# RWKV-7 rank-32 products as one split single-pass matmul with the terms stacked in the partitions

## The chip, the cores and the metric

The kernel runs on one core of a Trainium2 chip. The metric is the device time of one execution in microseconds (us). Before the change it is 1765.97 us, the median of two runs (1765.7 and 1766.24). The engines are named as the profile names them: PE (TensorE matmul), PEld (its weight load), DVE (VectorE), ACT (ScalarE), POOL (GpSimd) and SP (SyncE, which only issues DMAs). PSUM is the memory into which PE writes.

## The reference

One layer with two token mixers side by side and a gated MLP behind them, for 128 context tokens and 1024 latent tokens (1152 columns, d_model 1024). The part that changes is in the RWKV-7 mixer: decay and in-context learning rate come out of three products of rank 32.

```python
u_b = dwconv1d(u_b, p['rwkv_conv'])
r, k, v, wdf, wdb, ad, gd = jnp.split(u_b, idx, axis=-1)
w_f = jnp.exp(-DECAY_SCALE * jax.nn.sigmoid(p['rwkv_w0'][0] + jnp.tanh(wdf) @ p['rwkv_w2'][0]))
w_b = jnp.exp(-DECAY_SCALE * jax.nn.sigmoid(p['rwkv_w0'][1] + jnp.tanh(wdb) @ p['rwkv_w2'][1]))
a = jax.nn.sigmoid(p['rwkv_a0'] + ad @ p['rwkv_a2'])
```

`wdf`, `wdb` and `ad` have 32 channels each, `rwkv_w2` is 2 x 32 x 512 and `rwkv_a2` is 32 x 512. All is float32.

## The kernel before

**Stages.** Channels lie in the partitions and tokens in the columns. After the norm and the modulation, the input is kept twice, as `hh` (rounded to float32r, a float32 form that PE takes in one pass) and `hl` (the rest). A projection (`proj`, lines 1061 to 1073) loads 128 columns of a weight, splits them into `wh` and `wl` in the same way, and adds three single-pass products per 128 rows of the contraction and 384 tokens: `hh,wh`, `hl,wh` and `hh,wl` (lines 1070, 1071, 1072). So the large products already run in split form. The order of stages is: modulation and first columns; projections and features of four head pairs; HGRN2 and RWKV-7 scans; output projection; MLP.

**Features.** `features(p, r, k, v)` runs once for each of four pairs p and three blocks tb of 384 tokens, twelve blocks in all. In each block there are two places with rank-32 products. The first, which is called **a** here, is line 1331's input: `small_proj(wlora[64:96, cb], twt[64:96, c])`, one matmul with 32 contraction rows (it is recorded at line 1299). The second, called **dec** here, is a group of two such matmuls at line 1364, one for each direction, on partitions 0 to 31 and 32 to 63. Both operands are plain float32. `twt` (128 x 1152, memory `low`) holds the 96 features, and `wlora` (memory `fx`) the 96 rows of weights. Behind a and dec stand tanh on ACT, a scan and products on DVE, 24 small matmuls per direction (lines 1397 and 1398), and stores of the finished features. `elim` then inverts triangular systems: 31 pairs of steps on DVE (lines 1441 and 1444) and small matmuls (lines 1462 and 1464).

**What sets the order.** The program is first recorded as operations with their dependencies. Three tables then decide it: `SEQUENCE` is the order in which all operations are issued, `ENGINE_OF` names the engine where an operation has a choice (a copy on ACT, DVE or POOL; a store on POOL or SP), and `PLACE_OF` names the buffer. Each engine takes its instructions strictly in that order; semaphores hold them back. Memory is laid out by hand in large tiles (`low`, `top`, `fx`, `qm` and others); a name such as `ta` or `nb` is a place or two in one of them.

## Time and profile before

| what | value |
|---|---|
| median of the runs | 1765.97 us |
| profiled execution, its own time | 1769.48 us |
| span of the profiled execution | 1767.7 us |
| PE busy | 1708.6 us, 97% |
| PEld busy | 1539.8 us, 87% |
| DVE busy | 1434.8 us, 81% |
| ACT busy | 936.8 us, 53% |
| POOL busy | 350.5 us, 20% |
| mean granted PE clock | 0.998 |

The span runs from the first to the last instruction. A float32 matmul has two records in the profile, a float32r matmul one. Busy time of a group is the time in which at least one of its instructions ran. A row `L1299 PE MATMUL banks<-low,fx 32*128 32x384` is the operation of line 1299 on PE, writing PSUM (`banks`) from `low` and `fx`, with a weight of 32 rows and 128 columns and 384 moving columns. `low<-x` with an engine's q (SPq, POOLq) is a DMA issued there.

### The profile page before, as it was taken

Reading aid. Unit: us, or ns where it says so; the run is one execution under the profiler, and the core shown is the slowest. Engines: PE = TensorE matmul, PEld = TensorE weight load, DVE = VectorE, ACT = ScalarE, POOL = GpSimd, SP = SyncE. Lnnn points to the kernel's source line nnn. Section 1 sums busy time; section 2 is a strip of 40 time slices with the busy share of each in tenths; the row PEclk is TensorE's granted clock in tenths of the full one; section 3 lists DMA queues with packets and bytes.
Section 4 is the critical chain, followed back from the end, with each engine's and each line's share of the span. In section 5 each row is a group of like instructions: output and inputs, shape, how many; then the busy total and the mean of one; then the engine's idle time right before and its main releaser. Section 6 shows DMA issues by size and latency. Waiting matters only on the chain.

```text
span 1767.7 us, 44608 instructions
## 1 busy us (share of the span) xinstructions
PE 1708.6 (97%) x17726; PEld 1539.8 (87%) x17726; DVE 1434.8 (81%) x2742; ACT 936.8 (53%) x1955; POOL 350.5 (20%) x543
## 2 busy tenths in 40 slices
PE   6999999999999999999999999999999999999998
PEld 4888888888988888888778899999999999878787
DVE  5648889977779988886879797888988888878766
ACT  5657576663255656664556764444444444554542
POOL 0003141352222011112110122232333322000000
PEclk9999999999999999999999999999999999999999
DMA  8426365486777788989997757777877777896775
GB/s 278 137 72 164 89 162 139 112 232 195 203 207 221 212 246 278 288 271 289 296 288 264 215 122 153 155 157 160 165 156 153 146 162 149 282 306 218 229 231 183
DMA packets 342068, 352.97 MB, mean 200 GB/s; under 512 B 73180, under 2 KB 264565, under 8 KB 341508
## 3 DMA queue, kind: packets, MB, share of 16 engines
q1 hardware_dynamic: 287508, 282.27, 53.0%
q0 software_dynamic: 54352, 67.85, 19.6%
q8 instruction: 139, 2.28, 0.5%
q14 instruction: 69, 0.57, 0.1%
HBM read 254.99 MB, written 118.10 MB: 211 GB/s over the span
## 4 chain that ended last, share of the span: by engine, by line
PE 55%; DVE 18%; DMA 15%; issue 5%; ACT 4%; SPq 1%; POOL 1%; DVEq 0%; ACTq 0%; POOLq 0%
PE banks L2065 14%; PE banks L1070 6%; PE banks L1072 5%; PE banks L1071 5%; PE banks L2229 5%; DVE low L2153 3%; DMA low<-in_ffn_w_up_dram 2%; DMA wr<-in_ffn_w_down_dram 2%; PE banks L1955 1%; PE banks L1957 1%; PE banks L1956 1%; DMA d_t<-in_ffn_w_down_dram 1%; DMA low<-d_a 1%; DMA wr<-in_ffn_w_up_dram 1%; DMA wr<-d_o 1%
## 5 line engine op out<-in xcount | busy, mean ns | idle before, releaser
L1070 PE MATMUL banks<-hh,wh 128*128 128x384 f32 x768 | 278.5, 363 | 4.4 <-DVE fx L1250 3.1
L1072 PE MATMUL banks<-hh,wl 128*128 128x384 f32 x768 | 257.8, 336 | 0.0
L1071 PE MATMUL banks<-hl,wh 128*128 128x384 f32 x768 | 257.5, 335 | 0.0
L2153 DVE SCALAR_TENSOR_TENSOR low<-low,pf 128x1024 f32<-128x1024 f32 x176 | 225.4, 1281 | 7.9 <-ACT low L2147 5.2
L2065 PE MATMUL banks<-qm,wh 128*128 128x320 f32 x968 | 224.1, 310 | 0.2 <-ACT fx L2102 0.2
L2065 PE MATMUL banks<-hbm,wh 128*128 128x256 f32 x880 | 164.4, 283 | 3.6 <-DVE low L2123 1.9
L2065 PE MATMUL banks<-qm,wl 128*128 128x320 f32 x528 | 162.9, 308 | 0.2 <-DVE wl L2035 0.2
L1070 PEld LDWEIGHTS banks<-hh,wh 128*128 128x128 f32 x768 | 144.3, 188 | 20.5 <-issue 8.5
L2065 PEld LDWEIGHTS banks<-qm,wh 128*128 128x128 f32 x968 | 160.7, 189 | 0.5 <-ACT fx L2102 0.4
L1071 PEld LDWEIGHTS banks<-hl,wh 128*128 128x128 f32 x768 | 144.6, 188 | 2.7 <-issue 1.4
L1072 PEld LDWEIGHTS banks<-hh,wl 128*128 128x128 f32 x768 | 144.2, 188 | 0.0
L2065 PEld LDWEIGHTS banks<-hbm,wh 128*128 128x128 f32 x880 | 139.1, 190 | 5.2 <-DVE low L2123 2.5
L2065 PE MATMUL banks<-ham,wh 128*128 128x256 f32 (+1 forms) x616 | 132.0, 294 | 0.0
L2065 PE MATMUL banks<-hbm,wl 128*128 128x256 f32 x440 | 124.4, 283 | 0.6 <-DVE wl L2035 0.6
L2102 ACT COPY fx<-banks 128x256 f32<-128x256 f32 (+1 forms) x132 | 52.1, 398 | 108.1 <-PE banks L2065 101.3
L2065 PEld LDWEIGHTS banks<-ham,wh 128*128 128x128 f32 x616 | 101.5, 190 | 0.1
L2065 PEld LDWEIGHTS banks<-qm,wl 128*128 128x128 f32 x528 | 99.1, 188 | 0.6 <-DVE wl L2035 0.6
L2065 PEld LDWEIGHTS banks<-hbm,wl 128*128 128x128 f32 x440 | 83.9, 191 | 0.8 <-DVE wl L2035 0.8
L2173 POOL DMA_DIRECT2D d_t<-in_ffn_w_down_dram x44 | 45.0, 1050 | 183.9 <-DMA d_t<-d_t 139.9
L2035 ACT CAST wh<-wr 128x512 fp32r<-128x512 f32 x73 | 45.2, 622 | 66.2 <-PE banks L2065 28.6
L2035 ACT CAST wh<-low 128x512 fp32r<-128x512 f32 x81 | 50.0, 620 | 52.9 <-PE banks L2065 25.5
L2065 PE MATMUL banks<-ham,wl 128*128 128x256 f32 (+1 forms) x264 | 77.0, 292 | 0.0
(578 smaller groups left out, 4369.3 us busy)
## 6 DMA issues: line engine op xcount, KB each, us to landing
wr<-in_w_in_dram SPq DMA_DIRECT2D x34, 512.0 KB
d_t<-in_ffn_w_down_dram POOLq DMA_DIRECT2D x61, 256.0 KB, 5.8
low<-d_a SPq DMA_DIRECT2D x53, 256.0 KB
low<-d_ak SPq DMA_DIRECT2D x64, 192.0 KB
low<-d_kb SPq DMA_DIRECT2D x36, 256.0 KB
low<-in_ada_w_dram SPq DMA_DIRECT2D x32, 256.0 KB
fx<-in_ada_w_dram SPq DMA_DIRECT2D x16, 512.0 KB
top<-in_ada_w_dram SPq DMA_DIRECT2D x16, 512.0 KB
```

The source lines that it names most:

```text
L1070: mm(o, wh[:, kt, :], hh[:, kt, c], kt == 0, False)
L1071: mm(o, wh[:, kt, :], hl[:, kt, c], False, False)
L1072: mm(o, wl[:, kt, :], hh[:, kt, c], False, kt == KT - 1)
L1955: mm(ps, oh[:, kt, :], woh, kt == 0, False)
L1956: mm(ps, oh[:, kt, :], wol, False, False)
L1957: mm(ps, ol[:, kt, :], woh, False, kt == KT - 1)
L2035: split(*w, src)
L2065: pe.matmul(o, a[:, kt, :], b[:, kt, :], start=start and first, stop=last, skip_group_check=not start)
L2102: act.copy(keep[n], y[:, 0:w])
L2153: dve.scalar_tensor_tensor(av, shifted(dy, dx), tap(3 * dy + dx), av, MUL, ADD)
L2173: acc(td[j][k], b)
L2229: pe.matmul(o, x, y, start=fresh and f, stop=l, skip_group_check=not fresh)
```

## The change

The three terms of a split product (high by high, low by high, high by low) are put into the partitions, 32 rows each, so that one single-pass matmul with 96 contraction rows gives their sum.

- After tanh, the features of each token block are split: an ACT cast makes the high part and a DVE subtraction the low part. 27 stores (32 x 384 each, on POOL or SP) write them to a DRAM tensor `d_lo` in the order high, low, high for each of the three products.
- Each of the twelve blocks loads its 96 x 3 x 384 piece back into `lom` with a DMA on POOL. There is one such buffer, so the load of a block waits until dec of the block before has run.
- Each pair loads its 128 columns of `rwkv_w2` and `rwkv_a2` three times (six DMAs on SP), casts them on ACT into `w3` and subtracts on DVE in the third copy, which makes high, high, low. There is one buffer of `w3` in `lom` too.
- a and dec become one and two matmuls at line 1349 of the new kernel (function `lora`), all on partitions 0 to 95.
- `top` shrinks by 1536 columns to make room for `lom`; behind the features the same room is `topb`, and the first HGRN2 operation that may use it waits for all products (`lora_ops`). Some small buffers move; `wraw` has three places instead of four.
- All three tables are new.

```diff
@@ -120,337 +120,340 @@
 SEQUENCE = [int(i) for i in """
-0 12 13 14 11 2 15 16 27 1 17 18 19 4 20 22 28 29 33 3 24 30 39 23 31 32 34 35 36 40 37 38
...
@@ -795,7 +806,13 @@
-    top, qm = r1_.mem("top", N1), r1b.mem("qm", N1, F32R)
+    r1_.above.append(r2b)
+    top, qm = r1_.mem("top", NT1), r1b.mem("qm", N1, F32R)
+    lom, topb = r2a.mem("lom", NL, F32R), r2b.mem("topb", NL, box=r1_)
...
+    plan.tag("twt", [(lom, 0)], T)
+    plan.tag("wlora", [(lom, T)], 384)
...
@@ -1089,6 +1110,7 @@
+    lord = dram("d_lo", [96, 3, T])
...
@@ -1256,10 +1278,6 @@
-    wlora = tl("wlora", [P, 512])
-    for d in range(2):
-        ld(wlora[32 * d:32 * d + 32, :], I["rwkv_w2"][0, d])
-    ld(wlora[64:96, :], I["rwkv_a2"][0])
...
@@ -1293,6 +1311,14 @@
+    for tb in range(3):
+        c, lh, ll = slice(tb * 384, (tb + 1) * 384), tl("ta", [P, 384]), tl("nb", [P, 384])
+        act.copy(lh[0:96].bitcast(F32R), twt[0:96, c])
+        combine(ll[0:96].bitcast(F32R), twt[0:96, c], lh[0:96], SUB)
+        for j in range(3):
+            for a, t in enumerate((lh, ll, lh)):
+                st(lord[32 * a:32 * a + 32, j, c], t[32 * j:32 * j + 32, :])
+    lora_ops = []
...
@@ -1312,6 +1338,16 @@
+        raw3, w3 = tl("ta", [P, 3, P]), tl("wlora", [P, 3, P], F32R)
+        for a in range(3):
+            ld(raw3[32 * a:32 * a + 32, 0:2, :], I["rwkv_w2"][0].rearrange("d r c -> r d c")[:, :, cb])
+            ld(raw3[32 * a:32 * a + 32, 2, :], I["rwkv_a2"][0][:, cb])
+        act.copy(w3[0:96], raw3[0:96])
+        combine(w3[64:96], raw3[64:96], w3[64:96].bitcast(F32), SUB)
+
+        def lora(ps, j):
+            mm(ps, w3[0:96, j, :], lt[0:96, j, :], True, True)
...
@@ -1326,8 +1362,12 @@
+            lt = tl("twt", [P, 3, 384], F32R)
+            pool.dma_start(lt[0:96], lord[:, :, c].bitcast(F32R))
             ta, nb = tl("ta", [P, 384]), tl("nb", [P, 384])
-            ps = small_proj(wlora[64:96, cb], twt[64:96, c])
+            ps = pbank("sp")[:, 0:384]
+            lora(ps, 2)
...
@@ -1361,7 +1401,8 @@
-                    mm(dec[d], wlora[32 * d:32 * d + 32, cb], twt[32 * d:32 * d + 32, c], True, True)
+                    lora(dec[d], d)
```

**How the order moves.** On PE, in the first pair, dec of block 0 (two matmuls) and a of block 1 stand close together. `wh`, `wl`, `hh` and `hl` are the operands of a projection; between the rows shown only such projection matmuls stand, twelve in all before the change:

```order
L1072 MATMUL banks<-hh,wl_135 128x384
L1364 MATMUL banks<-low,fx 128x384 x2
L1070 MATMUL banks<-hh,wh_134 128x384
L1071 MATMUL banks<-hl,wh_134 128x384
L1072 MATMUL banks<-hh,wl_135 128x384
...
L1072 MATMUL banks<-hh,wl_135 128x384
L1299 MATMUL banks<-low,fx 128x384
```

After the change there are fifteen (lines 1091 to 1093 of the new kernel are 1070 to 1072 of the old):

```order
L1093 MATMUL banks<-hh,wl_137 128x384
L1349 MATMUL banks<-lom 128x384 x2
L1091 MATMUL banks<-hh,wh_134 128x384
L1092 MATMUL banks<-hl,wh_134 128x384
L1093 MATMUL banks<-hh,wl_137 128x384
...
L1093 MATMUL banks<-hh,wl_137 128x384
L1349 MATMUL banks<-lom 128x384
```

The distance has grown by three matmuls, and a now reads `lom`, which a DMA must have filled since dec.

On POOL, the loads of `lom` stand among the stores of the features and small copies. These are the rows around the loads for blocks 1 and 2 of the first pair (line 1320 stores to `d_lo`, 1399 stores the values, 1427 copies decay factors, 1464 and 1466 store features):

```order
L1320 DMA d_lo<-top 32x384 x3
L1366 DMA lom<-d_lo 96x3x384
L1399 DMA d_v_85<-top 128x3x128
L1427 COPY dcs<-top 128x6 x2
L1464 DMA d_kb_83<-top 64x6x128
L1416 MEMSET top 128x6
L1466 DMA d_kb_83<-top 64x6x64
L1366 DMA lom<-d_lo 96x3x384
```

Before the change the same stretch of POOL is this (1359 stores the values, 1386 copies decay factors, 1423 and 1425 store features):

```order
L1359 DMA d_v_84<-top 128x3x128
L1386 COPY dcs<-top 128x6 x2
L1425 DMA d_kb_82<-top 64x6x64
L1349 COPY top<-low 128x384
L1375 MEMSET top 128x6 x2
L1386 COPY dcs<-top 128x6 x2
L1423 DMA d_kb_82<-top 64x6x128
```

Each load of `lom` now stands in POOL's queue and holds what is behind it until PE has run dec.

More of the change, by code (lines that the diff above doesn't have):

```diff
@@ L463, in __init__, with mem @@
         self.tc, self.name, self.before, self.where, self.mems, self.pool = tc, name, before, where, [], None
-        self.under = under
+        self.under, self.above = under, []
+        if under:
+            under.above.append(self)
         self.left, self.end = 0, 0.0
-    def mem(self, name, n, dt=F32):
-        m = Mem(self, name, n, dt)
+    def mem(self, name, n, dt=F32, box=None):
+        m = Mem(box or self, name, n, dt)
+        m.owner, m.real = self, None
         self.mems.append(m)
@@ L473, in open @@
         if self.before:
+            for box in self.before.above:
+                if box.pool is not None:
+                    box.stack.close()
             self.before.stack.close()
@@ L635, in close @@
         reads, writes, op.tiles = [], [], set()
-        for m, a, k, _ in forms[0][1]:
-            w, r = self.operands(m, a, k)
-            writes += w
-            reads += r
+        for n, (_, l) in enumerate(forms):
+            for m, a, k, _ in l:
+                w, r = self.operands(m, a, k)
+                writes += [] if n else w
+                reads += r
         for ap in reads + writes + list(room):
@@ L1894, in step_kernel @@
             f, *a = rest.pop(0)
+            n0 = len(plan.ops)
             f(*a)
+            if len(rest) == 11:
+                for op in plan.ops[n0:]:
+                    op.deps.update(lora_ops)
             if a[1] == 2:
```

90 lines of the change are left out of this document (50 added, 40 removed), and 603 rows, old and new, of the table SEQUENCE.

## The prediction

> **What bounds the kernel now.** I read the page first (its busy times), then the table of stretches, then the groups of PE's instructions, then PE's timeline at two blocks.
>
> ```profile
> span 1767.7 us, 44608 instructions
> PE 1708.6 (97%) x17726; PEld 1539.8 (87%) x17726; DVE 1434.8 (81%) x2742; ACT 936.8 (53%) x1955; POOL 350.5 (20%) x543
> PE 55%; DVE 18%; DMA 15%; issue 5%; ACT 4%; SPq 1%; POOL 1%; DVEq 0%; ACTq 0%; POOLq 0%
> ```
>
> PE is busy for 97% of the span, and 55% of the chain that ended last is PE's. The features are made between about 75 and 420 us; the stretches there are the ones to look at.
>
> ```profile
> core 0: us, PE busy (x) PEld busy (x) DVE busy (x) ACT busy (x) POOL busy (x), PEclk, DMA share, GB/s
> 0.00:50.00 50.00, 34.32 (x237) 25.72 (x237) 30.38 (x89) 29.71 (x61) 4.09 (x20) 0.97 0.88 286
> ...
> 100.00:150.00 50.00, 49.96 (x366) 44.75 (x365) 30.86 (x47) 29.56 (x60) 7.50 (x14) 1.00 0.39 101
> 150.00:200.00 50.00, 49.34 (x451) 45.69 (x451) 44.53 (x100) 30.64 (x63) 10.84 (x23) 1.00 0.46 116
> 200.00:250.00 50.00, 48.98 (x753) 40.77 (x751) 42.31 (x77) 38.98 (x88) 23.21 (x40) 1.00 0.68 164
> 250.00:300.00 50.00, 48.12 (x544) 43.26 (x547) 45.96 (x90) 28.54 (x58) 7.60 (x19) 1.00 0.49 127
> 300.00:350.00 50.00, 49.92 (x523) 44.65 (x505) 46.27 (x100) 32.51 (x68) 18.20 (x32) 1.00 0.53 125
> 350.00:400.00 50.00, 49.65 (x774) 44.39 (x774) 39.89 (x80) 30.78 (x70) 26.45 (x48) 1.00 0.85 222
> 400.00:450.00 50.00, 46.37 (x488) 43.70 (x488) 38.51 (x85) 16.76 (x29) 9.67 (x16) 1.00 0.66 192
> ...
> sum 1000.00, PE 957.42 PEld 841.23 DVE 799.96 ACT 576.77 POOL 199.98; mean PE 47.87 PEld 42.06 DVE 40.00 ACT 28.84 POOL 10.00
> ```
>
> From 100 to 400 us PE leaves 4 us of 300 unused, at a full granted clock. What PE is spared here shortens the kernel, as long as nothing else steps into its place. The nearest candidate is DVE, at 92% between 250 and 350 us. The DMA engines are used to 39 to 68% until 350 us.
>
> **The change, part by part.**
>
> *The products on PE.* Their two groups, and PE's timeline at one a and one dec:
>
> ```profile
> L1299 PE MATMUL banks<-low,fx 32*128 32x384 f32 x24 | 10.9, 533 | 0.0
> L1364 PE MATMUL banks<-low,fx 32*128 32x384 f32 x48 | 11.6, 533 | 0.0
> ```
>
> ```profile
> 107.67 0.91 PE L1299 MATMUL banks<-low,fx 32*128 32x384 f32 x2
> 108.51 0.44 PE L1070 MATMUL banks<-hh,wh 128*128 128x384 f32 x1
> 108.79 0.34 PE L1071 MATMUL banks<-hl,wh 128*128 128x384 f32 x1
> ...
> 109.14 0.34 PE L1070 MATMUL banks<-hh,wh 128*128 128x384 f32 x1
> ...
> 110.88 0.33 PE L1071 MATMUL banks<-hl,wh 128*128 128x384 f32 x1
> ```
>
> ```profile
> 128.35 1.02 PE L1364 MATMUL banks<-low,fx 32*128 32x384 f32 x4
> 129.30 0.44 PE L1070 MATMUL banks<-hh,wh 128*128 128x384 f32 x1
> ```
>
> An a holds PE from 107.67 to 108.51, 0.84 us; a dec with its two matmuls holds it 0.95 us. Over twelve blocks the groups are busy 10.9 + 11.6 = 22.5 us. A single-pass matmul of 384 columns comes every (110.88 - 109.14) / 10 = 0.174 us. The 36 new matmuls have that form (384 columns, 128 weight columns) but 96 contraction rows, which no row here shows; the nearest row has 128. I take 0.174, so 6.3 us, and **16.2 us** are spared. Bounds: if each cost its own 0.34 us instead of the pitch, 12.2 us, and 10.3 are spared. Above, each float32 group also delays the next projection matmul: 108.79 - 108.51 is 0.28 instead of 0.174, so 0.1 us; 24 times 0.1 gives 18.6 spared.
>
> A rule of the Trainium skill speaks against this form: TensorE: Matmul & The Clock Gate, section "Why this matters for your kernels", says that a matmul of 32 contraction rows takes as long as one of 128 and that small ones should go to separate row groups so that they run at once. The trace agrees on the second half, since the two matmuls of dec take 0.95 us where one takes 0.84; by that rule alone the new dec would lose, two slots for one. What decides is the passes: 0.95 us against 2 x 0.174.
>
> *The loads of `lom`.* There is one buffer, so between dec of a block and a of the next one a POOL DMA must be issued, run and land, and PE stands if its own work in between is shorter; behind the waiting a stand projection matmuls that could run, but PE keeps its order, and ACT's tanh waits with it. That work, from the new order on PE, with the trace's durations for each kind:
>
> ```profile
> L1397 PE MATMUL banks<-top 64*32 64x64 f32 x576 | 17.0, 222 | 0.7 <-DVE top L1389 0.3 <-ACT low L1405 0.3
> L1462 PE MATMUL banks<-top 32*32 32x32 f32 x576 | 19.8, 228 | 0.0
> ```
>
> A pack of 24 feature matmuls is 17.0 / 24 = 0.71 us; 16 matmuls of an elimination are 19.8 / 36 = 0.55 us at most (36 x 16 records), and 32 of them some 1.0. With pN.m for the step from block m to m+1 of pair N: p0.0 has 15 projection matmuls, 2.6 us; p0.1 one pack and 6 projections, 1.75; p1.0 24 projections and 16 small, 4.6; p1.1 12, a pack and 32 small, 3.8; p2.0 18, 3.1; p2.1 21 and 48 small, 5.1; p3.0 21, 3.65; p3.1 6, a pack, three transposes and 48 small, 3.4. Between pairs there are over 160 matmuls, enough for anything.
>
> No load from DRAM into SBUF is issued by POOL in this part of the trace; the nearest rows are its stores (KB each, median us from issue to landing), and the spread of one line:
>
> ```profile
> d_g<-low POOLq DMA_DIRECT2D x3, 256.0 KB, 2.4
> d_ak<-top POOLq DMA_DIRECT2D x4, 384.0 KB, 4.3
> d_a<-low POOLq DMA_DIRECT2D x13, 576.0 KB, 5.0
> ```
>
> ```profile
> L1420 POOL DMA_DIRECT2D d_ak<-top x7: 772/854/882, 213.0 to 383.6; - x7
> DMA to landing us min/median/max: 2.4/3.9/6.5
> ```
>
> The new load is 96 x 3 x 384 x 4 bytes, 432 KB. I take 4.3 us, the row nearest in size and in the same stage; the ends are 2.4 and 6.5. The load starts when the second matmul of dec ends, 0.34 us after its start, and PE's other work starts 0.17 us after it, so a stall is 0.17 + landing - work. With 4.3: 1.9, 2.7, 0, 0.7, 1.3, 0, 0.8, 1.0, in all **8.4 us**. With 2.4 it is 0.8 us; with 6.5 it is 25 us.
>
> The Trainium skill has a fit for a DMA issued by POOL (DMA: Bandwidth & Descriptors, section "Anatomy of one DMA — SWDGE (gpsimd) path"): 2.0 us and the bytes at 436 GB/s, here an estimate of 3.0 us. The stalls would sum to 2 us and the time to about 1752. The trace's POOL rows lie above it (4.3 for 384 KB), except the quiet 2.4.
>
> *Behind the load on POOL* wait stores of features and copies of decay factors. They come from the same block whose dec is awaited or the one before, POOL is busy 7.5 to 26 us of each 50, and the buffers of those stores are double. I cost this at nothing; if the cover goes, the DVE products that refill `kb` and `kr` wait.
>
> *Splitting.* ACT and DVE each get seven more instructions; similar ones take
>
> ```profile
> 35.74 0.51 ACT L1198 CAST hh<-top 128x384 fp32r<-128x384 f32 x1
> 36.70 0.55 DVE L1199 TENSOR_TENSOR hl<-top,hh 128x384 fp32r<-128x384 f32 x1
> ```
>
> 3.6 us on ACT, which has 11 to 33 free us in each stretch, and 3.9 us on DVE, free 3.7 us or more in each. Nothing on the path. The 27 stores come before the first a: at 0.56 us each on POOL, 20 of them take 11 us,
>
> ```profile
> L1307 POOL DMA_DIRECT2D d_g<-low x3: 542/557/593, 81.5 to 100.4; - x3
> L1293 ACT ACTIVATE low<-low x1: 1170/1170/1170, 71.8 to 71.8; 64x1152 f32<-64x1152 f32 x1
> ```
>
> and start when tanh ends at 73.0 us plus the split; so by some 88 us, and with the load by 93, against 107.67 for the first a. The 24 small weight loads take SP's queue (three went away); SP's next weight load stands behind the last gate store, with about 10 us of PE work before its use. Nothing, by 3 us at worst.
>
> *The tables.* The main milestones stand where they stood: the first product of the scans moves from PE's matmul 3375 to 3323, the MLP's start does not move. DVE takes 68 copies more, ACT 39 and POOL 13 less. Nothing; bounds 9 us either way, a third of PE's idle time from 50 to 1000 us (950 less the 957.42 of the sum without the first stretch's 34.32, so 27 us).
>
> *Sum.* 1767.7 - 16.2 + 8.4 = 1759.9 us of span. The profiled execution took 1769.48, 1.8 more than its span, and lies 3.5 above the median; so 1759.9 + 1.8 - 3.5 = **1758 us**.
>
> **The rivals.**
>
> *Slower: the load of `lom` takes PE's place.* One mechanism: POOL's queue and a busy DMA make the landing longer than the work in each of the eight steps. It decides from a landing of 5.4 us, where the stalls reach 16.2. At 6.5 us, the longest in line 1420's row, the time is 1766 - 16 + 25 = 1775 us. For it: medians of 5.0 in this trace, steps of 1.75 to 3.8 us, and loads queued behind stores. Against: the DMA share is 0.39 to 0.68 until 350 us.
>
> *DVE becomes the bound.* Nine of twelve blocks lie past 150 us, where DVE is 80 to 93% busy, and it gets copies on top. Then what PE is spared turns into waits for DVE, and the time stays at 1766. Against it, DVE has idle time that is only alignment:
>
> ```profile
> DVE top L1324 <- ACT top L1323: 11.9, 2, 11.1
> DVE top L1378 <- ACT top L1376: 8.5, 6, 2.1
> ```
>
> *The tables win more.* Loads land in 3 us or less and the new order recovers 9 of the 27 idle us: 1766 - 16 + 2 - 9 = 1743 us.
>
> *The new matmuls aren't at the pitch.* With 0.34 us each, 1764 us.
>
> **How the numbers follow.** Forecast 0.50 (its own range 1750 to 1765), slower by the loads 0.20, DVE 0.12, tables 0.15, pitch 0.03. The ends are the bounds added: 1766 - 18.6 + 0.8 - 9 = 1739, and 1766 - 10.3 + 25 = 1781. This holds all cases but their tails. About 2% (35 us) is what a measurement of this kernel tells from no change. Faster by that, under 1731, needs more than all gains together: 0.07. Slower, above 1801, needs landings of 10 us in each step: 0.05. Within: 0.88.
>
> **What would show it.** The 36 matmuls at line 1349 should be busy 6 to 8 us in place of 22.5. PE should show waits for a DMA `lom<-d_lo` at line 1349 of some 8 us in all, most in the first pair, and the load's landing near 4.3 us. The HGRN2 and RWKV scans should start about 8 us earlier and the MLP's stretches be unchanged. If PE waits for DVE at lines 1397 or 1343's successors instead, DVE has become the bound. The forecast is wrong if the landing is under 3 or above 5.4 us, or if a stretch outside 75 to 420 us moves by more than 9 us.

## The result, and the profile after

The changed kernel is slower: 1813.61 us, the median of two runs (1809.45 and 1817.76), against 1765.97 us. The ratio is 1.0266, with a 95% interval of 1.0239 to 1.0293. The forecast was 1758 us, no change; the time lies above its range of 1739 to 1781 us. The profiled execution took 1817.76 us, with a span of 1815.8 us. Line numbers differ from kernel to kernel below, as edits move them. In the changed kernel line 1349 holds the new products, 1366 the load of the stacked features, 1091 to 1093 the projections (1070 to 1072 before), 1262 the store of an HGRN2 input.

The head of the page after, with the slices of PE and of its granted clock:

```profile
span 1815.8 us, 44579 instructions
PE 1720.8 (95%) x17690; PEld 1557.4 (86%) x17690; DVE 1456.5 (80%) x2810; ACT 918.8 (51%) x1916; POOL 392.5 (22%) x608
PE   7999998899968999999999999999999999999998
PEclk9999999999989999999999999999999999999999
```

PE is busy for 12 us more than before, though it has less to do, and its share fell from 97% to 95%. Each of the 40 slices is 45.4 us long. The seventh and eighth (272 to 363 us) and the twelfth and thirteenth (499 to 590 us) have lost. The table by stage says it in numbers (changed kernel, then before; the stretch, busy us and instructions of PE, PEld, DVE, ACT and POOL, then the granted clock, the DMA share and GB/s):

```profile
75.00:420.00 345.00, 318.53 (x3428) 289.09 (x3427) 267.62 (x533) 194.85 (x402) 109.41 (x202) 0.96 0.58 145
420.00:545.00 125.00, 107.36 (x1063) 101.39 (x1061) 79.83 (x167) 29.77 (x53) 35.59 (x60) 0.93 0.60 167
```

```profile
75.00:420.00 345.00, 337.22 (x3583) 299.18 (x3582) 277.10 (x544) 208.13 (x432) 95.52 (x177) 1.00 0.54 139
420.00:500.00 80.00, 80.00 (x881) 75.48 (x880) 55.29 (x113) 27.19 (x50) 25.00 (x43) 1.00 0.71 198
500.00:1000.00 500.00, 480.88 (x8036) 417.02 (x8036) 419.40 (x983) 292.84 (x681) 74.59 (x141) 1.00 0.86 263
```

From 75 to 420 us PE has no work for 26 us (345 - 318.53) where it had none for 8, and the mean granted clock is 0.96 in place of 1.00. Until 545 us, 18 us more go. How far the work has got is read best at the first matmul of the RWKV-7 recurrences, whose row gives the least, median and longest duration in ns and then the first and last start in us (before, then after):

```profile
L1786 PE MATMUL banks<-low x576: 222/222/222, 497.7 to 936.4; 128*64 128x64 f32 x192
```

```profile
L1827 PE MATMUL banks<-low x576: 221/222/271, 542.4 to 986.2; 128*64 128x64 f32 x192
```

The recurrences start 44.7 us later and end 49.8 later; what is behind them takes as long as before. So nearly the whole loss arises ahead of 545 us. There PE's largest waits in the changed kernel are these (us in total, times, the longest):

```profile
PE banks L1091 <- ACT fx L1264: 15.0, 1, 15.0
PE banks L1349 <- DMA lom<-d_lo: 12.9, 6, 4.1
```

The one at line 1349 was expected, though smaller (8.4 us). The one at line 1091, near 520 us, was not expected at all. ACT, for which PE waits there, itself waits for a store:

```profile
ACT fx L1261 <- DMA d_hv<-fx: 16.7, 1, 16.7
```

In the new order this store stands on SP behind the loads of four blocks of the bonus rows. There is one set of buffers for these blocks, so each block's loads wait until the stores of the block ahead have landed, the stores wait for DVE, and SP, which keeps its order, takes nothing else meanwhile. These are two of SP's waits from 480 to 545 us (line 1884 loads a block, 1891 and 1892 store to `d_vb`):

```profile
SPq L1884 <- DMA d_vb<-top: 7.9, 5, 2.2
SPq L1892 <- DVE top L1890: 6.5, 2, 3.6
```

One reload, as the timeline of the changed kernel shows it (start, length, engine; PE first, then POOL):

```profile
124.01 0.65 PE L1349 MATMUL banks<-lom 96*128 96x384 f32 x2
124.50 0.34 PE L1091 MATMUL banks<-hh,wh 128*128 128x384 f32 x1
...
126.93 0.34 PE L1093 MATMUL banks<-hh,wl 128*128 128x384 f32 x1
131.06 0.66 PE L1349 MATMUL banks<-lom 96*128 96x384 f32 x1 [3.79 <-DMA lom<-d_lo]
131.52 0.52 PE L1091 MATMUL banks<-hh,wh 128*128 128x384 f32 x1
131.84 0.52 PE L1092 MATMUL banks<-hl,wh 128*128 128x384 f32 x1
```

```profile
124.96 0.69 POOL L1366 DMA_DIRECT2D lom<-d_lo  x1 [37.45 <-PE banks L1349]
```

The matmul behind the decay products starts at 124.50, the next a starts at 131.06, and 15 projection matmuls, 2.6 us, lie in between, as the prediction counted. Behind the wait the projections follow one another at 0.32 us (131.52, 131.84) where they did at 0.17 us before it.

### The profile page after: what moved, and what is told of

The parts are those of the page before. It is cut to its first block, busy times and chain, and to the rows that moved or that the text cites. A ratio compares the mean times of both kernels' runs of the same rounds, so it can differ in the third digit from the quotient of the medians.

```text
span 1815.8 us, 44579 instructions
## 1 busy us (share of the span) xinstructions
PE 1720.8 (95%) x17690; PEld 1557.4 (86%) x17690; DVE 1456.5 (80%) x2810; ACT 918.8 (51%) x1916; POOL 392.5 (22%) x608
## 4 chain that ended last, share of the span: by engine, by line
PE 39%; DMA 5%; DVE 3%; issue 2%; ACT 1%; POOL 0%; SPq 0%; DVEq 0%; ACTq 0%; POOLq 0%
PE banks L2110 21%; PE banks L2274 12%; PE banks L2000 1%; PE banks L2002 1%; PE banks L2001 1%; DVE low L2198 1%; DMA wr<-in_ffn_w_down_dram 1%; DMA low<-in_ffn_w_gate_dram 1%; DMA low<-in_ffn_w_up_dram 1%; DVE wl L2080 1%; DMA wr<-in_ffn_w_up_dram 0%; DMA low<-in_ffn_w_down_dram 0%; DMA d_t<-in_ffn_w_down_dram 0%; DMA d_hg<-fx 0%; DMA fx<-in_ada_w_dram 0%
## 5 line engine op out<-in xcount | busy, mean ns | idle before, releaser
L1093 PE MATMUL banks<-hh,wl 128*128 128x384 f32 x768 | 263.0, 342 | 2.6 <-issue 2.6
L1092 PE MATMUL banks<-hl,wh 128*128 128x384 f32 x768 | 262.5, 342 | 0.0
L1091 PEld LDWEIGHTS banks<-hh,wh 128*128 128x128 f32 x768 | 148.4, 193 | 28.2 <-ACT fx L1264 16.5
L1092 PEld LDWEIGHTS banks<-hl,wh 128*128 128x128 f32 x768 | 148.8, 194 | 2.3 <-issue 1.4
L1093 PEld LDWEIGHTS banks<-hh,wl 128*128 128x128 f32 x768 | 148.0, 193 | 0.0
L2147 ACT COPY fx<-banks 128x320 f32<-128x320 f32 (+1 forms) x132 | 51.3, 397 | 97.2 <-PE banks L2110 90.1
L2218 POOL DMA_DIRECT2D d_t<-in_ffn_w_down_dram x44 | 49.2, 1173 | 71.7 <-DMA d_t<-d_t 40.3
```

The source lines that it names most:

```text
L1091: mm(o, wh[:, kt, :], hh[:, kt, c], kt == 0, False)
L1092: mm(o, wh[:, kt, :], hl[:, kt, c], False, False)
L1093: mm(o, wl[:, kt, :], hh[:, kt, c], False, kt == KT - 1)
L2147: act.copy(keep[n], y[:, 0:w])
L2218: acc(td[j][k], b)
```

## The experiments

Ratios are to the kernel before, timed beside each kernel, with 95% intervals. The changed kernel itself ran only twice, 8.3 us apart, so a gain over it of less than some 8 us is not clear of that spread. Starts, ends and waits are read from one profiled execution of each kernel.

**The wait for the load, the store on SP, and both.** The first kernel leaves out the eight loads of the second and third block of each pair:

```diff
             for op in self.order:
+                if op.id in (708, 763, 1168, 1223, 1628, 1683, 2088, 2143):
+                    continue
```

> This kernel is the changed one without the eight loads of the stacked features for the second and third stretch of each feature pair; it leaves out that these stretches get their own features, and computes them with those of the first. Nothing else is moved. Theory A (the loads): PE's idle time ahead of the new products (15.2 us in seven waits put down to the load, 12.4 us in five put down to nothing) goes for the eight stretches, and with it the lower granted clock behind each wait (0.80 to 0.90 at 130 to 150 and 210 to 230 us), so 25 to 35 us come off: 1778 to 1789 us. Theory B (the new tables are the loss): PE would wait there for the rest of the feature chain anyway, and at most 8 us come off: 1805 to 1814. In both, the 15.0 us that PE waits for ACT near 520 us stay.

Measured: 1798.33 us, 1.0168 (1.0132 to 1.0204). The waits at the products are gone, and some 15 us of time, less than the first theory said and more than the second. The wait for ACT near 520 us grew to 15.6 us. (The 15.2 and 12.4 us that the text above takes for PE's idle time add PE and PEld: PE's own waits for the load are the 12.9 us in six places shown before, and the 12.4 us are all PEld's.)

The second kernel moves two stores of that kind forward (2632 and 2656 are the stores, 2655 is a copy):

```diff
+        seq = list(SEQUENCE)
+        for ids, behind in [([2632], 2631), ([2655, 2656], 3129)]:
+            for i in ids:
+                seq.remove(i)
+            n = seq.index(behind) + 1
+            seq[n:n] = ids
+        self.order = [self.ops[i] for i in seq]
```

> This kernel is the changed one with two stores of the HGRN2 input projections taken out from behind the loads of the bonus rows on SP's queue: one now follows its copy directly, the other is moved with its copy 39 places forward. All is computed. Theory A (two separate losses): the 15.0 us wait of PE for ACT goes, and with it part of the low clock at 500 to 550 us (0.83 granted), so 15 to 22 us come off: 1791 to 1799 us. Theory B (the wait only shows a lateness that the recurrences, which start behind it, have from elsewhere): under 5 us come off: 1809 to 1814.

Measured: 1805.68 us, 1.0219 (1.0182 to 1.0257). The 15.0 us wait is gone, but only 7.9 us came off, no more than the spread of the changed kernel's own runs. The third kernel has both edits:

> Both edits together: no loads for the second and third stretches (these are computed with the features of the first, so their own are left out), and the two stores early. Theory A (two separate losses that add up): the sum of the two savings, 40 to 57 us, 1757 to 1774 us; the kernel is then the one before less 16 us of products plus what the tables cost elsewhere. Theory B (they overlap, the later wait absorbing the earlier lateness): no more than the larger of the two savings, 1778 or more.

Measured: 1799.11 us, 1.0173 (1.014 to 1.0206), the same as without the loads alone. The second theory holds: the savings overlap. PE's largest wait near 520 us in this kernel shows why:

```profile
PE banks L1833 <- DVE low L1818: 16.8, 1, 16.8
```

Line 1833 belongs to the recurrences and 1818 is a DVE step ahead of them. DVE's waits from 480 to 545 us have one large row, the bonus rows' loads of `d_v`, which still come one block after the other on SP:

```profile
DVE top L1895 <- DMA top<-d_v: 20.4, 5, 5.2
```

With the store out of the way, the same row of blocks holds PE by way of DVE. The second kernel has this wait too, with 16.7 us.

**PE kept busy.** Extra matmuls fill the wait for the load:

```diff
+            with plan.together():
+                for _ in range(20 if tb else 0):
+                    mm(ps, hh[:, 0, 0:P], hh[:, 0, 0:384], True, True)
                 lora(ps, 2)
```

> This kernel is the changed one with 20 extra single-pass matmuls of 384 columns, whose results nobody reads, ahead of the new product of the a term in each of the eight stretches with a fresh load: about 20 x 0.167 = 3.3 us of work for PE while it waits for the load. All else is as it was. Theory A (a wait of over 3 us costs the clock behind it as well): the matmuls fill the waits, the granted clock stays at 1.00 there, and 5 to 12 us come off: 1802 to 1809 us. Theory B (the clock is lower there for another reason, or its loss is covered): the time stays within 3 us of the changed kernel or grows by up to 10 where the matmuls outlast the wait: 1811 to 1824.

Measured: 1812.22 us, 1.0254 (1.0225 to 1.0284), no change. But most of the clock did come back. Three stretches of the changed kernel and of this one (the third number from the end is the granted clock):

```profile
125.00:150.00 25.00, 18.32 (x181) 16.98 (x180) 15.07 (x28) 12.15 (x27) 6.39 (x12) 0.89 0.70 173
200.00:225.00 25.00, 23.58 (x366) 20.97 (x364) 20.74 (x39) 14.60 (x33) 7.08 (x12) 0.86 0.58 137
275.00:300.00 25.00, 19.71 (x132) 17.73 (x130) 20.35 (x42) 13.46 (x28) 4.46 (x10) 0.93 0.39 91
```

```profile
125.00:150.00 25.00, 23.08 (x225) 21.94 (x223) 15.91 (x29) 12.38 (x27) 6.42 (x12) 1.00 0.67 173
200.00:225.00 25.00, 23.57 (x374) 21.46 (x374) 19.11 (x35) 13.99 (x32) 5.79 (x11) 0.93 0.51 122
275.00:300.00 25.00, 23.62 (x172) 21.09 (x174) 22.00 (x44) 13.90 (x29) 4.85 (x11) 1.00 0.40 95
```

So the waits do lower the clock behind them. From 200 to 225 us it stays at 0.93, so not all of the low clock is theirs. That the time stays is not evidence against it: 160 matmuls of about 0.17 us, some 27 us of work, were added to the features at no cost in time, twice the 12.9 us of waits that they could fill.

**The load a block ahead.** In the room of the one tile, two tiles; the a term's load of the next block then follows this block's a:

```diff
-    plan.tag("twt", [(lom, 0)], T)
+    plan.tag("twa", [(lom, 0)], 384)
+    plan.tag("twd", [(lom, 384)], 768)
...
-            pool.dma_start(lt[0:96], lord[:, :, c].bitcast(F32R))
+            with plan.aside():
+                pool.dma_start(la[0:96], lord[:, 2, c].bitcast(F32R))
+            pool.dma_start(ld_[0:96], lord[:, 0:2, c].bitcast(F32R))
```

The steps that are recorded `aside`, the loads of `la`, are then set behind a of the block ahead; `ld_` is loaded where the whole was.

> This kernel is the changed one with the stacked features in two tiles in the same room: one for the a term (384 columns), loaded for the next stretch as soon as this stretch's a product has read it, and one for the two decay terms (768 columns), loaded where the whole was. All is computed. Theory A (the wait for the load is one of two losses, and what lies near 520 us takes back about half of what is won there): the seven waits put down to the load go, and the time comes to that of the kernel without the loads, 1794 to 1803 us. Theory B (twice as many loads on POOL's queue hold each other up): 1806 or more.

Measured: 1807.79 us, 1.0237 (1.0211 to 1.0263), outside the first theory's range and in the second's. But its mechanism isn't what the profile shows: no wait for the load is left, and the wait near 520 us is there as before:

```profile
PE banks L1111 <- ACT fx L1284: 14.6, 1, 14.6
```

The gain of 5.8 us is less than the spread of the changed kernel's runs. Among the features PE now waits for DVE, at the product that is line 1343 of the kernel before (0.8 us there, 2.1 in the changed kernel):

```profile
PE banks L1405 <- DVE top L1401: 7.3, 6, 1.9
```

**The bonus rows later.** Five blocks are moved back to just ahead of their readers:

```diff
+        at = {i: n for n, i in enumerate(SEQUENCE)}
...
+        seq = sorted(SEQUENCE, key=at.get)
```

The lines left out give the nine operations of each of the blocks 1 to 5 new places from 4060, 4280, 4500, 4720 and 4940 on.

> This kernel is the changed one with five of the nine blocks of the bonus rows (blocks 1 to 5) moved some 1,300 to 2,000 places back in the order, to just ahead of the output stage that reads them; in the changed kernel they follow one another at about 480 to 530 us, with one set of buffers, each block waiting for the stores of the one ahead, on SP and on DVE. All is computed. Theory A (this row of blocks is the second loss: first it held a store of the HGRN2 inputs on SP, and with that store freed it held DVE ahead of the recurrences, 16.8 us in one wait): 15 to 28 us come off the changed kernel, with the low clock at 500 to 550 us: 1786 to 1799 us. Theory B (the recurrences start late for another reason): under 8 us come off, 1806 or more.

Measured: 1819.14 us, 1.0294 (1.0266 to 1.0322), no gain. Its row of the recurrences fits the mechanism, though the remedy fails:

```profile
L1834 PE MATMUL banks<-low x576: 222/222/270, 527.4 to 994.3; 128*64 128x64 f32 x192
```

They start 15.0 us earlier than in the changed kernel (527.4 for 542.4) and end 8.1 us later: so what is won ahead of the recurrences is lost again, and more, while they run with the blocks among them. With the two tiles as well:

> The split tiles and the five blocks moved back, together; all is computed. Theory A (the wait at the products and the row of bonus blocks are two losses, and nothing takes back the gain once both are gone): both savings in full, some 25 to 30 us for the products' waits with their clock and 15 to 28 for the blocks, 1756 to 1774 us. Theory B (a third loss in the new tables lies behind them): 1778 or more. Theory C (the products' gain is whole as well): below 1756.

Measured: 1809.55 us, 1.0242 (1.0218 to 1.0266). The recurrences start at 515.0 us and end at 980.4: again an early start, 27.4 us ahead of the changed kernel, and an end only 5.8 us ahead.

**What the shorter products are worth by themselves.** The kernel before, its tables unchanged, with single-pass products of another operand:

```diff
-            ps = small_proj(wlora[64:96, cb], twt[64:96, c])
+            ps = small_proj(hh[64:96, p, 0:P], hh[64:96, tb, 0:384])
...
-                    mm(dec[d], wlora[32 * d:32 * d + 32, cb], twt[32 * d:32 * d + 32, c], True, True)
+                    mm(dec[d], hh[32 * d:32 * d + 32, p, 0:P], hh[32 * d:32 * d + 32, tb, 0:384], True, True)
```

> This kernel is the one before with its 36 feature products as single-pass matmuls of the normalized input (32 rows of it, another weight and another stretch), at 0.175 us each in place of 0.625; it leaves out the real operands of these products, and has the tables, the room and the loads of before. Theory A (PE sets the pace between 75 and 420 us): the 16.2 us of PE work that the prediction removed come off, 1748 to 1754 us. Theory B (the products lay beside waits of PE for the feature chain, so that less work there only waits longer): under 5 us come off, 1762 or more.

Measured: 1768.84 us, 1.0003 (0.9984 to 1.0021). Nothing. The groups of the products in this kernel, and the row of the recurrences:

```profile
L1364 PE MATMUL banks<-hh 32*128 32x384 f32 x24 | 6.0, 457 | 0.0
L1299 PE MATMUL banks<-hh 32*128 32x384 f32 x12 | 5.3, 438 | 0.0
```

```profile
L1786 PE MATMUL banks<-low x576: 222/222/225, 495.3 to 943.5; 128*64 128x64 f32 x192
```

The products are busy for 11.3 us where they were for 22.5, but PE's busy time as a whole falls by only 2.8 us (1708.6 to 1705.8). The recurrences start 2.4 us earlier and end 7.1 us later. Where the rest went shows in part in the stage from 75 to 420 us (this kernel; the row before stands above) and in its two largest waits (this kernel, then before):

```profile
75.00:420.00 345.00, 335.33 (x3587) 303.82 (x3586) 279.13 (x547) 207.60 (x434) 96.64 (x180) 0.98 0.54 140
```

```profile
PE banks L1343 <- DVE top L1339: 2.4, 3, 1.7
PE banks L1070 <- DVE fx L1250: 2.3, 1, 2.3
```

```profile
PE banks L1070 <- DVE fx L1250: 3.1, 2, 1.6
PE banks L1343 <- DVE top L1339: 0.8, 1, 0.8
```

PE has no work for 9.7 us where it had none for 7.8: one wait for DVE has grown, the other has not. The granted clock takes more. It falls from 1.00 to 0.98, and 0.02 of 345 us is an estimate of up to 7 us. To see whether DVE is the one that sets the pace, its 24 decay scans (22.8 us) were left out, with the old products and with the short ones:

```diff
             for op in self.order:
                 e, l = op.forms[0]
+                if l[0][0] == 'tensor_tensor_scan' and l[0][1][0].shape[1] == 390:
+                    continue
```

> This kernel is the one before without the 24 prefix scans of the decay on DVE in the feature stretches (0.96 us each, 22.8 us in all); it leaves out the running sums of the decay, everything behind them is computed from the plain values. The 36 products are as before. Theory A (DVE, 88% busy between 125 and 400 us, paces the features together with PE): 6 to 15 us come off, 1752 to 1761. Theory B (PE alone paces them, as the prediction had it): within 4 us of before, 1763 to 1771. Theory C (the recurrences behind take back whatever the features win): the first scan starts earlier, and the time is still within 4 us.

> The kernel before with both: the 36 products as single passes of the normalized input (16.2 us less for PE) and without the 24 decay scans (22.8 us less for DVE); it leaves out the products' real operands and the running sums. Theory A (PE and DVE pace the features together, and only less of both is worth something): 10 to 16 us under the kernel that lost the scans alone, and clearly under before, 1740 to 1750. Theory B (PE alone): 16 us under before, 1748 to 1754, though the single passes alone came out even with before. Theory C (taken back behind): within 5 us of before, 1762 or more.

Measured: 1768.44 us, 1.0007 (0.9984 to 1.0029), and 1763.98 us, 0.999 (0.9971 to 1.0008). Both times fit theory C; the first alone fits theory B too. The recurrences of the two kernels (line 1788 here is line 1786 before):

```profile
L1788 PE MATMUL banks<-low x576: 222/222/222, 496.3 to 936.7; 128*64 128x64 f32 x192
```

```profile
L1788 PE MATMUL banks<-low x576: 222/222/225, 491.9 to 936.6; 128*64 128x64 f32 x192
```

With both taken away they start 5.8 us earlier, more than the two alone together (2.4 and 1.4), and end at 936.6 us where they ended at 936.4 before. This fits features that PE and DVE pace by turns, and a gain that is given back before 940 us. It isn't shown beyond that: each start is one execution, and the times of the kernel before alone spread from 1761 to 1773 us. What is shown is that less work for PE, for DVE or for both brings nothing clear of the interval.

**The bonus rows' room.** The layout of the changed kernel slides the features' tiles 1536 columns forward in `top`, to make the room of `lom`. The bonus rows' tiles stay, and come to lie over `ako` and `asys`, which the last pair's systems hold until just before the recurrences. This kernel puts them over `kr` and `kb`, and spreads blocks 0 to 5 over places 2470 to 2770 of the order, where they lay in 2734 to 2911 but for the first steps of block 0:

```diff
-    ... .add("hs", 2304).add("qyo", 768).add("sco", 384).add("vao", 384).add("g2", 384)
-    .add("on", 384).add("oss", 9, 2).add("pv", 512).add("pg", 512).add("lnr", 1024) ...
+    ... .add("hs", 2304).add("pv", 512).add("pg", 512).add("lnr", 1024)
+    .add("qyo", 768).add("sco", 384).add("vao", 384).add("g2", 384).add("on", 384).add("oss", 9, 2) ...
```

> This kernel is the changed one with the bonus rows' three tiles (2048 columns) moved in their part of the memory to the columns over kr and kb, which the last features leave early, in place of the columns over ako and asys, which the last triangular systems hold until the step before the recurrences; eight places in the order are pulled forward for it (six stores of kr and kb, the two loads of the norm's rows), and blocks 0 to 5 are spread over some 350 places before the recurrences, 60 apart, as they lay before. All is computed. Theory A (where the room put the bonus rows is the loss at 500 to 550 us): PE's time without work at 500 to 600 us falls to that of before and stays gone, 15 to 25 us come off the changed kernel: 1789 to 1799. Theory B (the blocks cost DVE and SP the same wherever they lie): under 8 us: 1806 or more.

> The same, and the stacked features in two tiles with the a term's load a stretch ahead. All is computed. Theory A (two losses that now add up): 25 to 40 us under the changed kernel, 1774 to 1789 us; what then remains against before is in the order of the rest. Theory B (each hides the other): no better than 1796.

Measured: 1800.45 us, 1.0201 (1.017 to 1.0233), and 1798.43 us, 1.0184 (1.0148 to 1.022). In the first the wait near 520 us is gone and 13 us come off. The second gains no more than its interval. Some 30 us over before remain, with neither a wait for the load nor the row of blocks. In the second kernel the recurrences still start at 526.1 us, 28.4 later than before, and PE's largest wait ahead of them is again the one for DVE at line 1343's product, 8.5 us in six places.

**The old order.** To part the new steps from the new tables, the tables were rebuilt from those of before: each step that both kernels have keeps its place, engine and buffer, and the new ones are set in behind what they need. The smaller room stays: `top` is 1536 columns shorter here too, and `wraw` has three places.

The new or changed steps are 113 with two tiles for the load. The layout, beside the two tiles:

```diff
+    ... .add("hs", 2304).add("qyo", 768).add("oss", 9, 2).add("pv", 512).add("pg", 512).add("lnr", 1024)
+    .add("sco", 384).add("vao", 384).add("g2", 384).add("on", 384).add("sm", 32, 2) ...
```

> The changed computation with the tables of before in place of the new ones: every step that both kernels have stands in the order, on the engine and in the buffer of before, the new steps (copies, stores, loads) are set in where what they need is done, and the bonus rows' and the features' tiles lie over one another as in before. The stacked features are in two tiles, the a term's load a stretch ahead. All is computed. Theory A (the new tables as a whole are the third loss, the 30 us that stay when loads and bonus rows are mended; the products are worth nothing): the time of before within 8 us, 1760 to 1775. Theory B (the new steps cost it: room, loads, stores, copies): 1785 or more. Theory C (the products count once the order is the old one): 1757 or less.

> The same with the stacked features in one tile, as the change has it: the load of a stretch's 432 KB is issued behind the decay products of the stretch before. All is computed. Theory A (the load's wait is a loss of its own whatever the order): 10 to 25 us over the kernel with two tiles, 1772 to 1795. Theory B (the wait shows only where the new order leaves little work in between): within 5 us of it.

> As the kernel with two tiles and the old order, but with the first 455 places of the order (the normalization of the input, until about 60 us) as the new tables have them, since the changed kernel came out of that stage 3 to 5 us earlier than the one before. All is computed. Theory A (that lead is kept where the order behind it is the old one): 2 to 5 us under the two-tile kernel with the old order. Theory B (it is absorbed, like the shorter products): the same time within 2 us.

Measured: 1785.23 us, 1.0099 (1.0069 to 1.0128); with one tile 1821.06 us, 1.03 (1.0274 to 1.0327); with the new order's first part 1788.04 us, 1.0095 (1.0058 to 1.0132). For the first, this is the edge of theory B: the new steps or their room cost some 18 us with the old tables too. The new order's first part brings nothing. The one-tile kernel is the change with the old tables, and it is no faster than the change with its own. Its wait for the load and the landing:

```profile
PE banks L1425 <- DMA lom<-d_lo: 28.8, 7, 6.4
DMA to landing us min/median/max: 4.1/5.3/7.4
```

Two tiles take 36 us off in this order (1821.06 to 1785.23, past the range of its theory A), though they took about 6 off in the new one. What is left, 18 us, has one large single wait in the two-tile kernel:

```profile
PE banks L1408 <- issue: 8.5, 1, 8.5
```

This is the first gate product, at 79 us. The copies and differences of the features stood ahead of the gate's last steps, on ACT and DVE. The last two kernels move them: first behind the gate's tanh, then also apart from one another. The order of these steps:

```diff
-tanh(twt), copy 0, copy 1, copy 2, tanh(sgt), gates
+tanh(twt), tanh(sgt), copy 0, copy 1, copy 2, gates
+tanh(twt), tanh(sgt), copy 0, gates 1 to 3, copy 1, gates 4 to 7, copy 2, gates 8 and 9
```

> The kernel with the old order and two tiles, but with the copies and differences of the features and their 27 stores set behind the gate's tanh on ACT; in the kernel with the old order they stood ahead of it, and PE stood idle for 8.5 us at 79 us ahead of the first gate product. All is computed. Theory A (of the 18 us over before, this wait is about half, and the rest are the new steps spread over the features): 7 to 10 us under the kernel with the old order, 1774 to 1779. Theory B (the lead is absorbed like that of the shorter products): within 3 us of it, 1782 or more. Theory C (nothing but this wait stands between it and the products' gain): below 1765.

> As the last kernel (old order, two tiles, gates first), with the second and third of the three copies of the features set a few gate products later, so that the stores behind the copy before have landed when they come, and the first pair's weights loaded later, so that both of their buffers are free for the copies. In the last kernel ACT waited 9.5 us in two places for stores out of two buffers, and PE 8.4 us for ACT. All is computed. Theory A (these waits of ACT, one after the other, are the half of what is left): PE's time without work at 50 to 100 us falls from 14 to under 5 us, and the time to 1774 to 1782. Theory B (absorbed behind): the wait goes and the time stays at 1785 or more.

Measured: 1791.13 us, 1.0134 (1.0084 to 1.0183), and 1792.17 us, 1.0159 (1.0121 to 1.0196). In the first, PE's wait only moved, to a projection that waits for ACT (first row), which waits for the stores out of its two buffers (second row, of ACT's waits):

```profile
PE banks L1168 <- ACT low L1374: 8.6, 2, 8.4
```

```profile
ACT top L1393 <- DMA d_lo<-top: 9.5, 2, 5.6
```

In the second PE still waits for ACT at two gate products, 3.3 us at 87 us and 2.9 at 105, and the time is no better. The stretches 50 to 100 and 100 to 420 us of the kernel with the old order, and of this one:

```profile
50.00:100.00 50.00, 41.48 (x235) 36.28 (x235) 23.30 (x56) 27.31 (x53) 9.43 (x24) 0.93 0.42 116
100.00:420.00 320.00, 303.17 (x3398) 279.42 (x3398) 255.66 (x501) 198.90 (x418) 109.36 (x197) 0.97 0.60 153
```

```profile
50.00:100.00 50.00, 46.61 (x260) 40.92 (x259) 21.98 (x51) 27.72 (x56) 7.56 (x20) 0.97 0.35 106
100.00:420.00 320.00, 299.65 (x3381) 277.21 (x3380) 258.32 (x507) 197.65 (x416) 110.06 (x201) 0.97 0.61 155
```

PE wins 5.1 us of work before 100 us and loses 3.5 by 420, 2.9 of these in that second wait. Both kernels end in their theory B.

## Why the prediction was wrong

**"Products 16.2 us off the path": failed, twice over.** First the size: the nearest row that I took for the new matmul was the pitch of projections in a row, 0.174 us. A lone product between other work holds PE longer, 0.25 us from the start of an a to the next matmul (286.97 to 287.22 in the changed kernel) and 0.49 us for the two of a dec (124.01 to 124.50). The records of the 36 are busy for 13.9 us in the changed kernel and 11.3 in the kernel before with short products, not 6.3; the sum had set a pitch for the new ones against busy time for the old:

```profile
L1349 PE MATMUL banks<-lom 96*128 96x384 f32 x36 | 13.9, 435 | 13.8 <-DMA lom<-d_lo 12.9 <-ACT top L1395 0.8
```

Second, and this decides: the step "what PE is spared here shortens the kernel", read from PE's share of 97%, failed. The run with only the shorter products gives 1.0003 (0.9984 to 1.0021). In its profile longer waits and a lower clock took most of it back in the features, and the next stage the rest. The rival "DVE becomes the bound" had the right time for this term and names its sign rightly: where the wait for the load is gone, PE waits for DVE at line 1343's product, 7.3 us for 0.8. As a mechanism it was half: less DVE work gives nothing either, and less of both only starts the recurrences 5.8 us earlier.

**"Loads 8.4 us": right mechanism, too small.** The landing came out as taken (4.3, 4.6, 5.1 us for least, median, most; 4.3 was predicted), and the work in between nearly so. What failed is the formula 0.17 + landing - work: it let the landing begin at the end of the products. In the reload shown above POOL begins to issue 0.46 us after the next matmul has started, issues for 0.69 us, and a starts 6.56 us after it where the formula has 4.47. Over the eight reloads PE stood 3.79, 2.13, 0, 0.61, 4.11, 0, 0.32 and 1.97 us, where the prediction has 1.9, 2.7, 0, 0.7, 1.3, 0, 0.8 and 1.0. So the term measured 12.9 us for 8.4. Even the kernel without these loads takes 1798.33 us, so they are at most some 15 of the 48 us lost.

The rival "the load takes PE's place" was to decide from a landing of 5.4 us, with stalls of 16.2. It didn't come to that: the median landing was 4.6 and the stalls 12.9. The Trainium skill's fit (DMA: Bandwidth & Descriptors, section "Anatomy of one DMA — SWDGE (gpsimd) path"), an estimate of 3.0 us for this load, lies under all the landings measured here.

**The clock: missing from the sum.** Behind a wait of 3.79 us the projections ran at 0.32 us for 0.17, the clock was 0.89 from 125 to 150 us, and with the waits filled it was 1.00. The Trainium skill states this (TensorE: Matmul & The Clock Gate, section "HAM oscillation — how this bites in real kernels": no idle gap of PE over about 3.4 us, or what follows runs at half the clock); the trace agrees for this wait. The measurement goes further than that rule: waits of 2.13 and 1.97 us (ending at 146.51 and 385.98) were followed by some 3 us at 0.32 too. Nor does the drop always come at once; behind the longest wait for the load three projections still started at the old pitch:

```profile
286.97 0.41 PE L1349 MATMUL banks<-lom 96*128 96x384 f32 x1 [4.11 <-DMA lom<-d_lo]
...
287.81 0.52 PE L1091 MATMUL banks<-hh,wh 128*128 128x384 f32 x1
```

The rule spoke against this change more than the one on 32 rows that I weighed. What the clock cost can be estimated from PE's busy time: it grew by 12.2 us (1708.6 to 1720.8) although the products are busy for 8.6 us less, so the rest of its work took some 21 us more, an upper estimate, since only a part of that lay on the path.

**"Tables: nothing, within 9 us": wrong in its parts.** The new order and room put six blocks of the bonus rows into one row before the recurrences. The store behind them on SP made PE wait 15.0 us; with that store moved it was DVE and 16.8 us; with the blocks spread in other room, the wait was gone and 13 us came off. I had looked at milestones in PE's order, which don't move when SP's order does. The 68 copies that went to DVE were counted but priced at nothing: DVE is busy for 21.7 us more (1434.8 to 1456.5), and no run parts what that costs. As a whole, though, the new tables did not lose against the old ones for this change: 1.0266 (1.0239 to 1.0293) against 1.03 (1.0274 to 1.0327) with one tile.

**"Splitting and 27 stores: nothing."** In the changed kernel this held: its first features are ready early. In the old order it did not: wherever the copies were set, PE stood for 3 to 9 us at a time between 79 and 108 us.

**The end: the scans should have started 8 us earlier.** They started 44.7 us later. The prediction's own sign for that, a stretch outside 75 to 420 us that moves by more than 9 us, came true at 420 to 545 us. That the MLP's stretches would not change was right.

**The sum.** The gap between 1758 and 1813.61 us is 56 us. What the runs show of it is 16.2 for the products that gave nothing, some 7 for the loads (15.3 gained without them, 8.4 predicted) and 13 for the bonus rows, 36 in all; but the gains of the runs overlap, so even these don't add up strictly, and the rest stays open.

**What stays open.** The two-tile kernel in the old order is still 18 us over before. Its loss too lies ahead of the recurrences, which start at 518.5 us, 20.8 later than before. The wait of 8.5 us was tried, and moving it brought nothing. Not tried were its waits for DVE, of which these are the largest from 75 to 560 us (some 18 us with the smaller ones, where before has 6):

```profile
PE banks L1461 <- DVE top L1457: 4.0, 4, 1.8
PE banks L1168 <- DVE fx L1349: 4.0, 2, 2.5
PE banks L1426 <- DVE top L1473: 2.6, 1, 2.6
```

Nor was its granted clock: 0.93 and 0.97 in the rows of 50 to 100 and 100 to 420 us above, 1.00 before, an estimate of up to 13 us (0.07 of 50 and 0.03 of 320). Whether the new steps or their smaller room make DVE late there is not parted by any run. Why a lead of 6 us at 490 us is gone by 940 us isn't settled either: in that stage PE is busy for 96% of the time, DVE for 84%, and the DMA share is 0.86 (480.88, 419.40 and 0.86 in the row of 500 to 1000 us above), so none of the three has much room, and no run here took work from that stage. How much of the changed kernel's loss is the clock alone isn't known, since the run that restored it also added 27 us of work to PE. No version tried is faster than the kernel before by more than its interval.

## What to carry to other kernels

Where two engines are some 80% busy or more in the stages concerned, as here, what one engine is spared is not yet time: test it by the cheapest stand-in first (here one edit of two lines gave 1.0003), before room, loads and tables are bent for it. A single buffer that is refilled from DRAM costs the whole way from the last reader to the next one (release, the issuing engine's turn, issue, landing), not the landing (6.56 us for 4.6 in one reload), and behind waits of 2 to 4 us PE's work ran at half its pace for a while; a second piece in the same room took 36 us off in one order and 6 in the other. After a new order is made, look at what stands in a row on the DMA-issuing queues behind a single set of buffers, not only at the busy engines.

## What the runs showed of the hardware

The granted clock fell behind waits of 1.97 to 4.11 us for the load and rose again: the pitch of projections was 0.17 us before such a wait and 0.32 us for some 3 us behind it, at once or about 1 us later, and stretches of 25 us among the features came to 0.86 to 0.93; twenty matmuls without a reader in each wait brought most of them back to 1.00. A wait of 2.00 us for ACT (ending at 319.60) was not followed by it. The load of 432 KB from DRAM issued by POOL landed in 4.3 to 5.1 us in the changed kernel and in 4.1 to 7.4 us in the old order; the same bytes in two loads landed in 2.4 to 4.9 us (144 KB) and 3.5 to 5.8 us (288 KB) in the kernel with two tiles and the new order. The single-pass product of 384 columns is busy for a mean of 435 to 457 ns in the records, at 32 and at 96 rows alike, while projections of the same columns follow one another at 0.17 us.
